# Three elementwise operations moved from GpSimd to VectorE in a two-layer trunk with three attention branches

## Chip, cores and metric

The kernel runs on one core of a Trainium2 chip. The metric is device time in microseconds of one execution; the median of the runs is what counts. Engines are called as the profile calls them: PE is TensorE, DVE is VectorE, ACT is ScalarE, POOL is GpSimd and SP is SyncE, which here only issues DMAs.

## The reference, cut to what matters

Two layers (DEPTH 2) work on x of 1 x 256 x 1024 in float32. Each takes h = RMSNorm(x) and projects it at once to all that the three attention branches need; MoBA has 6 heads, NSA 4, FoX 6, all of 64 columns.

```python
def hybrid_layer(x, ...):
    h = rms_norm(x, norm_g)
    proj = h @ w_in
    ...
    # NSA: per head, three gated outputs are summed (compressed, selected, window)
    return gc[..., 0:1] * o_c + gc[..., 1:2] * o_s + gc[..., 2:3] * o_w
    ...
    y_moba = (o_moba * jax.nn.silu(mz)) @ w_up_moba     # silu(z) = z * sigmoid(z)
    y_nsa = (o_nsa * jax.nn.silu(nz)) @ w_up_nsa
    y_fox = (o_fox * jax.nn.silu(fz)) @ w_up_fox
    g = jax.nn.sigmoid(gl + b_gate).reshape(B, S, N_BRANCH, D_MODEL)
    merged = g[:, :, 0] * y_moba + g[:, :, 1] * y_nsa + g[:, :, 2] * y_fox
    return x + merged @ w_out
```

## The kernel before, in words

The 256 rows are two tiles of 128 partitions (t = 0, 1). Every large product is made in three passes of 32-bit matmuls on split operands: a weight tile `st` comes by DMA on SP's queue, ACT copies it to the high part `wh` (L262), DVE subtracts to get the low part `wl` (L263), and PE runs `wh` with the high activations, `wl` with the high ones, `wh` with the low ones (`mm3`, L287 to L289). Split tiles are prepared four tiles ahead (`prefetch`, `part`).

A layer goes: projections of the branches with their head work; scores, softmax and values of the heads (`attend`) while PE also makes the six gate products (`mm_gl`); then the gate stage (`gate_out`), the lift with the merge (`mm_up`), and the output product (`mm_out`).

The order on PE is written out. Its instructions are emitted by generators on a hand-kept clock (`tick`, `unit`, `finish`, with lags such as LAG_K) and the kernel asks for a manual schedule of PE alone. The instructions of DVE, ACT and POOL are not held to the order in which the code emits them: the framework sorts each of these queues when the program is built, by order of emission among what it takes to be ready. On the chip every queue then runs strictly in that order. The two places where the change and PE meet most closely are a chain and a ring. The chain is in `cmp_heads`: PE transposes the compressed probabilities, DVE copies them to `pc` (L850), PE multiplies them with the values (L857). On DVE's queue the second of two sums on `ck` (L909, which waits for a DMA that goes through DRAM) and a weight split stand ahead of `pc`. The ring is the PSUM pool `pat` of three tiles, all named `at`, which scores (L565, L566), transposes of queries and keys (L473) and transposes of probabilities (L579) use in turn; L494 to L496 read the transposed keys and so free a tile.

Three places work on POOL and are touched. In `gate_out`, for each half c of the 1024 columns and each t, ACT makes the sigmoid of z into a buffer `tmp` (L937), POOL multiplies z by it (L940), DVE multiplies the head outputs `om` by that (L941); PE transposes the products later (`transpose_split`, L336). In `mm_up`, for each half n and branch b, DVE multiplies the accumulator by the gate (L974 for b = 0, L977 for the others) and adds it to `mg` (L978): POOL does so for b = 1, DVE for b = 2. In `gated`, which closes an NSA branch, DVE multiplies the values in the PSUM bank `o` by 1/sum times gate (L666 for the first branch, L670 for the two others), and for these POOL adds the result to `om` (L671). `gated` is called three times in a layer: for the selected branch (first), for the window branch, and in `cmp_heads` for the compressed one. Buffers named `tmp` form a ring of four, which the loads of `b_gate` on SP's queue (L917) use too.

Of the kernel before, what the change touches and what calls it, by code (L numbers as in the profile page):

```python
# [9 lines left out]
F32 = mybir.dt.float32  # L10
F32R = mybir.dt.float32r
AF = mybir.ActivationFunctionType
ALU = mybir.AluOpType
# [3 lines left out]
S, D, L, HD = 256, 1024, 2, 64  # L17
# [5 lines left out]
MH, NH, FH = 6, 4, 6  # L23
# [70 lines left out]
def trunk(ctx, tc, x, w_in, b_gate, cmp_w1, w_up_moba, w_up_nsa, w_up_fox, w_out, gains_d, eye_d, x_t, small_d, row_d, out):  # L94
    nc = tc.nc
    V, A, G, T = nc.vector, nc.scalar, nc.gpsimd, nc.tensor
# [13 lines left out]
    wk = ctx.enter_context(tc.tile_pool(name="wk", bufs=2))  # L110
# [66 lines left out]
    def after(i, others):  # L177

        for o in others:
            tc.add_manual_dep(i.ins, o.ins.name, nosync, reason="one table set after the other")  # L180
# [40 lines left out]
    def finish(*us):  # L221
        while any(u["done"] is None for u in us):
            tick(0.25)
# [67 lines left out]
    def new_acc():  # L291
        return [pacc.tile([128, 512], F32, name="acc") for _ in range(NT)]

    def dense(ps, act, parts, n, half=0, ks=None, order=None, oldest=None):

        whole = ks is not None or len(parts) == KD
        ks = list(ks) if ks is not None else [half * 4 + i for i in range(len(parts))]
        for i, t in order or [(i, t) for i in range(len(parts)) for t in range(NT)]:
            h, lo = part(parts[i], oldest and (oldest if t < NT - 1 else parts[i]))
            k = ks[i]  # L300
            first = i == 0 if whole else k == 0
            last = i == len(parts) - 1 if whole else k == KD - 1
            mm3(ps[t][:, 0:n], block(act, 0, k, t), block(act, 1, k, t), h, lo, first, last)
            tick(3 * n * 0.00042)
# [16 lines left out]
    def new_T():  # L321

        return [(pgs.tile([128, 4, S], F32R, name="hT", tag="page"),
                 pgs.tile([128, 4, S], F32R, name="lT", tag="page")) for _ in range(2)]
# [4 lines left out]
    def transpose_split(dst, t, blocks, gains=None):  # L329

        n = len(blocks)
        h, lo = [d[:, :, t * 128:(t + 1) * 128] for d in dst]
        ps = pat.tile([128, 512], F32, name="at")
        p3 = ps[:, 0:n * 128].rearrange("p (k c) -> p k c", k=n)
        for k in range(n):
            T.transpose(p3[:, k, :], blocks[k], ident)  # L336
        if gains is not None:
            f = wk.tile([128, 4, 128], F32, name="tmp", bufs=4)[:, 0:n]
            V.tensor_tensor(f, p3, gains[:, :, None].to_broadcast([128, n, 128]), op=ALU.mult)
            p3 = f  # L340
        A.activation(h, p3, AF.Copy)
        V.tensor_tensor(lo, p3, h.bitcast(F32), op=ALU.subtract)

    def blocks_of(a, k0, n):
        return [a[:, k * 128:(k + 1) * 128] for k in range(k0, k0 + n)]
# [4 lines left out]
    def layer(l):  # L350
# [307 lines left out]
        def gated(bank, rsum, b, first=False):  # L658

            V.reciprocal(rsum, rsum)  # L660
            V.tensor_tensor(rsum, rsum, sh["ng"].rearrange("p t (h b) -> p t h b", b=3)[:, :, :, b], op=ALU.mult)
            for t in range(NT):
                o = sh["om"][t][:, 384:640].rearrange("p (h d) -> p h d", d=HD)
                g = rsum[:, t, :, None].to_broadcast([128, NH, HD])
                if first:
                    V.tensor_tensor(o, bank[:, t], g, op=ALU.mult)  # L666
                else:
                    tmp = wk.tile([128, 512], F32, name="tmp", bufs=4)
                    o1 = tmp[:, 0:256].rearrange("p (h d) -> p h d", d=HD)
                    V.tensor_tensor(o1, bank[:, t], g, op=ALU.mult)  # L670
                    G.tensor_tensor(o, o, o1, op=ALU.add)  # L671

        def nsa_heads(b, v):
            def head(h, bank, rsum):
                return attend(sh["nqs"][:, h, :], [sh[n][:, b, :] for n in ("kh2", "kl2")], lambda kt: sh[v][:, kt, :],
                              h, bank, h, rsum)
            return group(4, head, lambda bank, rsum: gated(bank, rsum, b + 1, b == 0))
# [146 lines left out]
        def cmp_heads():  # L824
# [31 lines left out]
            for t in range(NT):  # L856
                T.matmul(bank[:, t].rearrange("p h d -> p (h d)"), pcs[t], sh["vcb"].rearrange("p h d -> p (h d)"),  # L857
                         start=True, stop=True)
            gated(bank, wc, 0)
            turn[2] = clock[0] + LAG_B  # L860

# [67 lines left out]
        def gate_out(c):  # L929

            if c == 0:
                sh["oT"] = [tuple(qkp.tile([128, 4, S], F32R, name="qkT") for _ in range(2)) for _ in range(2)]
            for t in range(NT):
                s_ = wk.tile([128, 512], F32, name="tmp", bufs=4)
                zc = sh["z"][t][:, c * 512:(c + 1) * 512]
                oc = sh["om"][t][:, c * 512:(c + 1) * 512]
                i = A.activation(s_, zc, AF.Sigmoid)  # L937
                after(i, exps)
                sigs.append(i)
                G.tensor_tensor(zc, zc, s_, op=ALU.mult)  # L940
                V.tensor_tensor(oc, oc, zc, op=ALU.mult)  # L941
            yield 6.5 + 4.5 * c
            for t in range(NT):
                transpose_split(sh["oT"][c], t, blocks_of(sh["om"][t], c * 4, 4))
                yield 1.0
# [15 lines left out]
        def mm_up(n, parts, before):  # L961

            if n == 0:
                sh["mg"] = [pgs.tile([128, D], F32, name=f"mg{t}", tag="page") for t in range(NT)]
                sh["mT"] = new_T()
            for b, (k0, k1) in enumerate(((0, 3), (3, 5), (5, 8))):
                finish(*before.get(b, ()))
                ps = new_acc()
                dense(ps, sh["oT"], parts[k0:k1], 512, ks=range(k0, k1))
                for t in range(NT):  # L970
                    g = sh["gl"][t][b][:, n * 512:(n + 1) * 512]
                    m = sh["mg"][t][:, n * 512:(n + 1) * 512]
                    if b == 0:
                        V.tensor_tensor(m, ps[t], g, op=ALU.mult)  # L974
                    else:
                        tmp = wk.tile([128, 512], F32, name="tmp", bufs=4)
                        V.tensor_tensor(tmp, ps[t], g, op=ALU.mult)  # L977
                        (G if b == 1 else V).tensor_tensor(m, m, tmp, op=ALU.add)  # L978

        def merged_T(n):  # L980
            yield 3.0
# [90 lines left out]
        def run(starts, following):  # L1072
# [51 lines left out]
            for c in range(5):  # L1124
                mm_gl(c, sh["gls"][c])
            finish(*every)
            g0, g1 = unit(gate_out(0)), unit(gate_out(1))
            unit(gate_sig(0))
            unit(gate_sig(1))
            mm_gl(5, sh["gls"][5])  # L1130
            unit(gate_sig(2))
            mm_up(0, sh["ups"][0], {0: [g0], 1: [g1]})
            m0 = unit(merged_T(0))
            mm_up(1, sh["ups"][1], {})
            m1 = unit(merged_T(1))
            finish(m0)
# [41 lines left out]
```

## Time and profile before

| | |
|---|---|
| median of 3 runs | 518.33 us (518.25 to 518.99) |
| the profiled execution | 517.28 us |
| its span | 515.5 us, 8244 instructions |
| PE busy | 501.9 us, 97% |
| DVE busy | 401.5 us, 78%, 846 instructions |
| ACT busy | 334.6 us, 65% |
| POOL busy | 60.5 us, 12%, 84 instructions |

The profile times single instructions in one execution. The span runs from the first instruction to the last; the execution's own time is 1.8 us longer, and the medians are taken from other executions. An engine's busy time is an average over stages with different limits, so a stage is read from its own stretch. Idle time on an engine is given with what ended it. Consecutive instructions of one kind may stand in one row of the timeline (x2), with the time from the first start to the last end. Durations on an engine can overlap a little: one instruction may start before the one before it is written out.

### The profile page before, as it was taken

The page shows a single profiled execution, that of the slowest core. Times are in us where ns is not written, and L with a number is a line of the kernel's source. Part 1 is how long each engine was busy: PE and PEld are TensorE (multiplying, and loading weights), DVE is VectorE, ACT ScalarE, POOL GpSimd, SP SyncE. Part 2 cuts the span into 40 slices and gives each one's busy share as a digit, 9 for nine tenths or more (in the row PEclk, how much of TensorE's full clock was granted, in tenths as well). Part 3 has the DMA queues.
Part 4 walks back from the last instruction along what each step waited for, and adds up shares of the span by engine and source line. Part 5 has one row for each costly group of instructions (what it writes and reads, how often), then busy time and mean ns, then how long its engine had stood idle before and what let it go on. Part 6 is the DMA issues. An engine that isn't in the chain of part 4 may idle for free.

```text
span 515.5 us, 8244 instructions
## 1 busy us (share of the span) xinstructions
PE 501.9 (97%) x2822; PEld 446.6 (87%) x2822; DVE 401.5 (78%) x846; ACT 334.6 (65%) x645; POOL 60.5 (12%) x84
## 2 busy tenths in 40 slices
PE   8899999999999999999999999999998999999997
PEld 6788999999788888888889989999987888888886
DVE  4799988789876658998497998768997755698953
ACT  4887676976675576654276976678757666655440
POOL 3510211000110005025100000000011000042300
PEclk9999999999999999999999999999999999999999
DMA  8999886555585443756557898647556643537502
GB/s 279 332 243 256 237 246 194 148 166 162 164 257 144 124 129 116 219 163 190 144 145 207 202 244 268 173 127 202 154 182 189 194 130 116 164 117 226 180 9 81
DMA packets 60226, 93.09 MB, mean 181 GB/s; under 512 B 3980, under 2 KB 34840, under 8 KB 60184
## 3 DMA queue, kind: packets, MB, share of 16 engines
q1 hardware_dynamic: 56592, 89.67, 59.7%
q10 hardware_dynamic: 3592, 2.90, 1.7%
q8 instruction: 22, 0.36, 0.3%
q14 instruction: 20, 0.16, 0.1%
HBM read 91.49 MB, written 1.06 MB: 180 GB/s over the span
## 4 chain that ended last, share of the span: by engine, by line
PE 81%; DVE 8%; ACT 5%; DMA 3%; issue 3%; ACTq 0%; DVEq 0%; SPq 0%
PE acc L287 22%; PE acc L289 21%; PE acc L288 21%; DVE wl L263 4%; PE at L579 2%; DMA st<-in_w_in_dram 2%; ACT wh L262 2%; PE at L565 2%; PE at L566 2%; PE at L336 1%; PE o L587 1%; PE o L589 1%; PE o L591 1%; PE at L473 1%; PE o L768 1%
## 5 line engine op out<-in xcount | busy, mean ns | idle before, releaser
L263 DVE TENSOR_TENSOR wl<-st,wh 128x1024 fp32r<-128x1024 f32 (+4 forms) x180 | 200.3, 1120 | 53.7 <-ACT wh L262 52.0
L262 ACT ACTIVATE wh<-st 128x1024 fp32r<-128x1024 f32 (+4 forms) x180 | 170.2, 953 | 86.9 <-PE acc L289 68.0
L287 PE MATMUL acc<-wh,hT 128*128 128x512 f32 (+4 forms) x560 | 216.8, 387 | 1.4 <-ACT wh L262 1.0
L288 PE MATMUL acc<-wl,hT 128*128 128x512 f32 (+4 forms) x560 | 202.6, 362 | 0.9 <-DVE wl L263 0.9
L289 PE MATMUL acc<-wh,lT 128*128 128x512 f32 (+4 forms) x560 | 203.0, 362 | 0.0
L289 PEld LDWEIGHTS acc<-wh,lT 128*128 128x128 f32 x560 | 105.1, 188 | 10.9
L287 PEld LDWEIGHTS acc<-wh,hT 128*128 128x128 f32 x560 | 105.8, 189 | 9.2 <-ACT wh L262 1.4
L288 PEld LDWEIGHTS acc<-wl,hT 128*128 128x128 f32 x560 | 105.9, 189 | 7.8 <-DVE wl L263 1.5
L574 ACT ACTIVATE p<-p,nm 128x128 f32<-128x128 f32 x80 | 35.6, 446 | 24.4 <-DVE nm L572 24.3
L940 POOL TENSOR_TENSOR z<-z,tmp 128x512 f32<-128x512 f32 x8 | 12.9, 1645 | 109.0 <-ACT tmp L937 109.0
L287 PE MATMUL acc<-wh,qkT 128*128 128x512 f32 x64 | 25.6, 400 | 0.0
L289 PE MATMUL acc<-wh,qkT 128*128 128x512 f32 x64 | 25.0, 391 | 0.0
L288 PE MATMUL acc<-wl,qkT 128*128 128x512 f32 x64 | 25.0, 390 | 0.0
L978 POOL TENSOR_TENSOR mg<-mg,tmp 128x512 f32<-128x512 f32 x8 | 15.8, 1997 | 51.5 <-DVE tmp L977 51.5
L579 PE MATMUL at<-ident,p 128*128 128x128 f32 x120 | 19.8, 274 | 0.3
L926 DVE SCALAR_TENSOR_TENSOR gl<-acc,rt,tmp 128x512 f32<-128x512 f32 x24 | 17.3, 745 | 1.8 <-PE o L591 1.1
L579 PEld LDWEIGHTS at<-ident,p 128*128 128x128 f32 x120 | 15.0, 146 | 2.5 <-ACT qkT L496 0.6
L572 DVE CUSTOM_DVE_ANT_0 p<-at,tabs 128x128 f32<-128x128 f32 (+1 forms) x56 | 17.0, 354 | 0.1
L583 DVE COPY pt<-at 128x384 f32<-128x384 f32 x20 | 11.1, 555 | 7.2 <-PE at L579 7.0
L768 PE MATMUL o<-wh,Z 128*63 128x256 f32 x64 | 15.6, 282 | 0.4 <-DVE Z L744 0.3
L581 ACT ACTIVATE pt<-at 128x384 f32<-128x384 f32 x20 | 9.7, 483 | 9.5 <-PE at L579 9.4
L769 PE MATMUL o<-wl,Z 128*63 128x256 f32 x64 | 15.4, 280 | 0.2 <-DVE wl L263 0.2
(238 smaller groups left out, 690.9 us busy)
## 6 DMA issues: line engine op xcount, KB each, us to landing
st<-in_w_in_dram SPq DMA_DIRECT2D x52, 512.0 KB, 3.6
st<-in_w_in_dram SPq DMA_DIRECT2D x56, 384.0 KB, 4.1
st<-in_cmp_w_dram SPq DMA_DIRECT2D x32, 256.0 KB, 4.7
st<-in_w_out_dram SPq DMA_DIRECT2D x16, 512.0 KB, 3.8
st<-in_w_in_dram SPq DMA_DIRECT2D x8, 396.0 KB, 6.9
st<-in_w_in_dram SPq DMA_DIRECT2D x8, 390.0 KB, 3.2
tmp<-in_b_gate_dram SPq DMA_DIRECT2D x12, 256.0 KB, 4.4
st<-in_w_up_moba_dram SPq DMA_DIRECT2D x4, 512.0 KB, 3.6
```

What stands on the lines that cost most here:

```text
L262: return (lambda: A.activation(h, s_, AF.Copy), lambda: V.tensor_tensor(lo, s_, h.bitcast(F32), op=ALU.subtract))
L263: lambda: V.tensor_tensor(lo, s_, h.bitcast(F32), op=ALU.subtract))
L287: T.matmul(ps, sh, wh, start=first, stop=False)
L288: T.matmul(ps, sh, wl, start=False, stop=False)
L289: T.matmul(ps, sl, wh, start=False, stop=last)
L572: V.tensor_tensor_reduce(out=u, in0=sp, in1=add[t], scale=-SCALE, scalar=BIG, op0=ALU.add, op1=ALU.min, accum_out=nm)
L574: exps.append(A.activation(u, u, AF.Exp, bias=nm, scale=-1.0, accum_out=rsum[:, t, hb:hb + 1]))
L579: T.transpose(pts[:, s * 128:(s + 1) * 128], p[:, s * 128:(s + 1) * 128], ident)
L768: T.matmul(U, st, h, start=i == 0, stop=False)
L769: T.matmul(U, st, lo, start=False, stop=i == CL - 1)
L926: V.scalar_tensor_tensor(sh["gl"][t][b][:, n * 512:(n + 1) * 512], ps[t], sh["r"][:, t:t + 1], bg, op0=ALU.mult, op1=ALU.add)
L978: (G if b == 1 else V).tensor_tensor(m, m, tmp, op=ALU.add)
```

## The change

The product of z and its sigmoid, and the sum of the second branch, are given to DVE. The NSA sum becomes one DVE operation per head, which multiplies by the head's factor and adds to `om`; a group of two products on 128x256 and two sums becomes eight operations on 128x64, and its two `tmp` buffers are no longer taken.

```diff
@@ gated
             for t in range(NT):
                 o = sh["om"][t][:, 384:640].rearrange("p (h d) -> p h d", d=HD)
-                g = rsum[:, t, :, None].to_broadcast([128, NH, HD])
                 if first:
-                    V.tensor_tensor(o, bank[:, t], g, op=ALU.mult)
-                else:
-                    tmp = wk.tile([128, 512], F32, name="tmp", bufs=4)
-                    o1 = tmp[:, 0:256].rearrange("p (h d) -> p h d", d=HD)
-                    V.tensor_tensor(o1, bank[:, t], g, op=ALU.mult)
-                    G.tensor_tensor(o, o, o1, op=ALU.add)
+                    V.tensor_tensor(o, bank[:, t], rsum[:, t, :, None].to_broadcast([128, NH, HD]), op=ALU.mult)
+                    continue
+                for h in range(NH):
+                    V.scalar_tensor_tensor(o[:, h], bank[:, t, h], rsum[:, t, h:h + 1], o[:, h], op0=ALU.mult, op1=ALU.add)
@@ gate_out
-                G.tensor_tensor(zc, zc, s_, op=ALU.mult)
+                V.tensor_tensor(zc, zc, s_, op=ALU.mult)
                 V.tensor_tensor(oc, oc, zc, op=ALU.mult)
@@ mm_up
-                        (G if b == 1 else V).tensor_tensor(m, m, tmp, op=ALU.add)
+                        V.tensor_tensor(m, m, tmp, op=ALU.add)
```

## Rows read from the trace of the kernel before

**Rows 1.** The page, busy us (share of the span) and instructions:

```profile
PE 501.9 (97%) x2822; PEld 446.6 (87%) x2822; DVE 401.5 (78%) x846; ACT 334.6 (65%) x645; POOL 60.5 (12%) x84
```

**Rows 2.** PE's waits: who for whom, us in total, times, longest:

```profile
PE o L857 <- DVE pc L850: 2.6, 2, 1.5
```

**Rows 3.** Stretches: length, busy us (instructions) of PE, PEld, DVE, ACT, POOL, clock, DMA:

```profile
126.00:146.00 20.00, 18.81 (x103) 15.38 (x102) 17.41 (x52) 12.54 (x35) 3.19 (x5) 1.00 0.61 192
146.00:196.00 50.00, 50.00 (x289) 43.20 (x289) 30.39 (x68) 32.96 (x67) 0.00 (x0) 1.00 0.52 153
196.00:232.00 36.00, 36.00 (x172) 29.73 (x171) 33.19 (x38) 22.23 (x26) 9.93 (x6) 1.00 0.57 166
232.00:256.00 24.00, 24.00 (x112) 19.88 (x111) 15.91 (x20) 8.52 (x9) 8.95 (x6) 1.00 0.61 179
...
448.00:484.00 36.00, 36.00 (x172) 29.84 (x171) 33.24 (x39) 20.99 (x26) 9.92 (x6) 1.00 0.54 169
```

**Rows 4.** Groups of POOL: busy us, mean ns of one, idle before them:

```profile
L978 POOL TENSOR_TENSOR mg<-mg,tmp 128x512 f32<-128x512 f32 x8 | 15.8, 1997 | 51.5 <-DVE tmp L977 51.5
L940 POOL TENSOR_TENSOR z<-z,tmp 128x512 f32<-128x512 f32 x8 | 12.9, 1645 | 109.0 <-ACT tmp L937 109.0
...
L671 POOL TENSOR_TENSOR om<-om,tmp 128x256 f32<-128x256 f32 x8 | 5.7, 739 | 66.7 <-DVE rs_a L318 54.9 <-DVE tmp L670 11.8
```

**Rows 5.** Timeline, gate stage of the first layer, DVE, then PE (start, us):

```profile
200.13 3.48 DVE L941 TENSOR_TENSOR om<-om,z 128x512 f32<-128x512 f32 x2 [1.19 <-POOL z L940]
...
205.76 1.28 DVE L941 TENSOR_TENSOR om<-om,z 128x512 f32<-128x512 f32 x2
...
210.01 0.60 PE L336 MATMUL at<-ident,om 128*128 128x128 f32 x4
```

**Rows 6.** Timeline, merge of the first layer's first half, DVE, then PE:

```profile
227.36 1.28 DVE L978 TENSOR_TENSOR mg<-mg,tmp 128x512 f32<-128x512 f32 x2
...
229.63 0.60 PE L336 MATMUL at<-ident,mg 128*128 128x128 f32 x4
```

**Rows 7.** DVE's scalar_tensor_tensor from PSUM: two groups, and a timeline row:

```profile
L503 DVE SCALAR_TENSOR_TENSOR kl<-at,tabs,kh 128x128 fp32r<-128x128 f32 x8 | 2.6, 347 | 0.1
...
L871 DVE SCALAR_TENSOR_TENSOR xf<-acc,rt,row 128x6 f32<-128x6 f32 x4 | 0.9, 224 | 1.1 <-PE acc L289 1.1
...
44.27 0.61 DVE L503 SCALAR_TENSOR_TENSOR kl<-at,tabs,kh 128x128 fp32r<-128x128 f32 x2
```

**Rows 8.** Timeline, DVE, second NSA group of the first layer:

```profile
141.75 0.75 DVE L670 TENSOR_TENSOR tmp<-o,wc 128x256 f32<-128x256 f32 x2
```

**Rows 9.** Timeline, first layer: the PSUM ring behind that group:

```profile
140.63 0.55 DVE L583 COPY pt<-at 128x384 f32<-128x384 f32 x1
...
141.23 0.33 PE L565 MATMUL at<-qkT 128*128 128x128 f32 x1 [0.17 <-DVE pt L583]
...
143.40 0.40 ACT L574 ACTIVATE p<-p,nm 128x128 f32<-128x128 f32 x1 [1.98 <-DVE nm L572]
...
152.25 0.58 ACT L496 ACTIVATE qkT<-at,tabs 64x384 fp32r<-64x384 f32 x1 [0.24 <-DVE klT_fk L495]
...
153.79 0.30 PE L565 MATMUL at<-qkT 128*128 128x128 f32 x1
```

**Rows 10.** Timeline, first layer: DVE ahead of `pc`, and PE's wait for it:

```profile
137.09 0.96 DVE L909 TENSOR_TENSOR ck<-ck,tabs 128x768 f32<-128x768 f32 x1 [1.72 <-DMA ck<-csd]
137.96 1.22 DVE L263 TENSOR_TENSOR wl<-st,wh 128x1024 fp32r<-128x1024 f32 x1
139.10 0.48 DVE L850 COPY pc<-at 128x128 f32<-128x128 f32 x2
...
139.44 1.13 PE L857 MATMUL o<-vcb,pc 128*128 128x256 f32 x4 [1.03 <-DVE pc L850]
```

## The prediction

> **What bounds the kernel now.** I read the busy times first. PE is busy 501.9 of 515.5 us, 97%, while POOL, from which the change takes work, is busy 12% [rows 1]. So the end is set by PE's fixed order, and the change can move the time only by opening or closing a gap on PE. The view of PE's own waits comes second: what the reader is to see there is how short it is. Past the start of each layer one entry is left, two waits of PE for `pc` on DVE, 2.6 us in all, the longer 1.5 [rows 2], the shorter 1.03 [rows 10]. Third, the stretches that hold the three edited places. From 146 to 256 us PE is busy all the time, and in the second layer's gate stage again [rows 3]: nothing that DVE or POOL does there ends a wait of PE. Only the stretch from 126 to 146 us, where the NSA sums run, has PE below its whole length, 18.81 of 20.00, with DVE busy 17.41. The NSA sums are therefore the part that can show; the other two sit under a full PE.
>
> **The gate products (eight, L940).** Removed: eight POOL instructions of 1645 ns, 12.9 us of POOL [rows 4], and DVE's 1.19 us of waiting for the first of them in each layer [rows 5]. Added: eight DVE instructions on 128x512 with all operands in SBUF. The nearest row is the same shape and kind at L978, two in 1.28 us [rows 6], 0.68 for one and 0.60 from one start to the next. Per layer that adds 4 x 0.60 = 2.4 us to DVE. Given back: the two L941 that run beside POOL take 3.48 us where the two after it take 1.28 [rows 5], so 2.2 us, and the wait of 1.19. DVE comes through about 1.0 us earlier (1.19 + 2.2 - 2.4). Could it be a loss? The second half's products end at 205.76 + 1.28 = 207.04, and PE does not begin the transposes even of the first half before 210.01 [rows 5]. So 2.97 us of cover stand behind a change of about -1.0, and a gain has no reader, since PE reaches these transposes in its own order with no gap. Term: 0, from above and below. Without that cover a late product would cost PE its whole lateness.
>
> **The sums of the merged branches (eight of sixteen at L978).** Removed: eight POOL instructions of 1997 ns, 15.8 us [rows 4]. Added: 2 x 0.60 = 1.2 us of DVE for each half of the columns. The second branch is added ahead of the third, so the worst is that all 1.2 us come through to the third branch's sums. The first of those ends at 227.36 + 0.68 = 228.04, PE's transposes of `mg` start at 229.63 [rows 6]: 1.59 us of cover. Term: 0. A gain again finds PE full [rows 3]. The hidden side effect, less waiting of weight loads on SP's queue for buffers, shortens nothing that PE waits for. No DMA is added or moved, and POOL, left with its zero fills and rotary tables, gets to them no later.
>
> **The NSA sums (L670, L671).** There are four such groups, two in each layer. Removed per group: two DVE products from PSUM, 0.75 us for two [rows 8], and two POOL sums of 739 ns [rows 4]. Added: eight DVE instructions, each 128x64, one input in PSUM, one in SBUF, a scalar per partition. The trace has this operation at 6 columns (224 ns) and at 128 columns (347 ns) [rows 7]. Between them 64 columns cost 224 + 58 x (347 - 224)/122 = 282 ns. From start to start it is less: two L503 take 0.61 us together [rows 7], 0.08 less than twice 347 ns, so DVE starts the next one 0.08 us before the last ends. I take 0.20 us from one to the next, 1.60 for eight. The two products that go away hold DVE 0.75 - 0.08 = 0.67. **Each group lengthens DVE's queue by 0.93 us.** The bounds: 0.14 us each (224 less 0.08), so 1.15 for eight, +0.5; and 0.282 each with no overlap, 2.26, +1.6. What is queued behind?
>
> The first group of a layer has scores and a weight split behind it, and then `ck` (L909), before which DVE stands idle for 1.72 us, waiting for a DMA, until 137.09 [rows 10]. 0.93, and even 1.6, ends in that idle time, and `wl` and `pc` behind it start when they do now. PE's wait for `pc` stays. Term: 0.
>
> The second group, at 141.75, is behind `pc` and ahead of the scores of two MoBA heads. ACT waits for those (1.98 us before 143.40) and then works its queue off, up to L496 at 152.25, which frees a PSUM tile of the `at` ring at 152.25 + 0.58 = 152.83. PE asks for that tile at 153.79 [rows 9]: 0.96 us later. The hand-over itself takes 0.05: `pt` ends at 140.63 + 0.55 = 141.18 and PE starts at 141.23 [rows 9]. So 0.91 us is free, 0.93 is added: 0.02 us of new wait, 0.04 for the two layers. This is the tightest cover in the change.
>
> [...]
>
> **The sum.** 0 + 0 + 0 + 0.04 = 0.04 us on the profiled execution, 517.28 us (515.5 of span and 1.8 around it), so 517.32. That execution lies 1.05 below the median of the three runs, 518.33. Moved to the median: 518.4 us, no change that shows. About 0.2%, 1.0 us, is what a measurement of this kernel can tell from none.
>
> **Rivals.** First, **slower through the PSUM ring**. If the eight small instructions do not overlap (each waiting for the one before, since all write parts of one `om` tile), a group adds 2.26 - 0.67 = 1.59 us, 0.68 more than the 0.91 free, in both layers: 1.4 us, 519.7. It decides once one instruction takes more than (0.67 + 0.91)/8 = 0.20 us from start to start. Against it: successive instructions overlap in the row at hand [rows 7]. For it: the margin is almost exactly used up. Chance 0.14. [...]
>
> Second, **faster through `pc`**. Only PE's order is written out; DVE's queue is put in order anew when the program is built, from what is then thought ready. In the present order `pc` stands behind `ck`, late by its DMA, and a split `wl` whose place costs 139.10 - 137.96 = 1.14 us [rows 10]. Eight instructions for two can tip that order. If `pc` comes ahead of `wl` in both layers, 1.03 goes whole and at least 1.14 of the 1.5; if ahead of `ck` too, both go: 2.6 us, 515.8. Chance 0.18: the wait is there, but nothing in the edit aims at it.
>
> Third, **slower through `pc`**: the same re-ordering puts one more split, or the second pair of scores, between `ck` and `pc`. Priced at one split, 1.14 in each layer, 2.3 us: 520.7. Chance 0.12.
>
> That the products leave POOL is written in the edit and can't fail to happen. That POOL's share hid something of use, so that the whole 34 us of it came off the span, is ruled out by the full PE [rows 3].
>
> **How the numbers follow.** No change has 0.56, and its own range is 517.9 to 518.9: the lower bound of the small instruction gives 0, the rest is the spread of the runs. Faster has 0.18, slower 0.14 + 0.12 = 0.26. For 8 in 10 the range goes from the faster rival's 515.8 to just past the third rival's 520.7, so 521.0; beyond it lie re-orderings that set several instructions in front of `pc`.
>
> **What would show it.** POOL falls by 12.9 + 15.8 + 5.7 = 34 us to about 26. DVE's L941 are all 0.68 us. The small instructions read about 0.28 us, eight of them 1.7 us from the first start to the last end. PE's waits still list `pc` with about 2.6 us, and L565 after each second group starts without a new wait. In the gate stage PE is busy all the time, with the transposes at the same distance. A time off by over 1 us means that `pc`'s entry has changed, or that a wait for a PSUM tile of the `at` ring has come up near 154 us and at its counterpart in the second layer; a new gap under the gates or the sums would prove the cover there misread.

## The result: 1.0% slower, and the profile after

The changed kernel takes 523.74 us, the median of 4 runs (522.43 to 524.82), against 518.34: a ratio of 1.010, 95% interval 1.0073 to 1.0128. The forecast was 518.4, no change, with 515.8 to 521.0 as its range; the result lies outside. The profiled execution took 522.43 us with a span of 520.6, so 5.15 us more than the one of before.

The page's busy times, to be held against [rows 1]:

```profile
PE 505.0 (97%) x2822; PEld 450.0 (86%) x2822; DVE 404.8 (78%) x886; ACT 334.6 (64%) x645; POOL 26.3 (5%) x60
```

POOL has lost its 34 us and stands at the 26 forecast. DVE has gained only 3.3 us. Neither tells why PE is later. PE's own waits do (us in total, times, longest):

```profile
PE at L579 <- DVE nm L572: 6.1, 2, 3.4
```

The two waits for `pc` of [rows 2] are gone from the list. In their place PE waits twice for `nm` at L579, the transposes of probabilities: 6.1 us where it was 2.6. The stretches of [rows 3], with the same columns, and the second layer's counterpart of the first one as the fifth row:

```profile
126.00:146.00 20.00, 17.30 (x88) 14.09 (x88) 15.75 (x53) 9.93 (x25) 0.31 (x1) 0.91 0.54 165
146.00:196.00 50.00, 50.00 (x286) 43.04 (x286) 32.19 (x78) 34.53 (x75) 0.00 (x0) 1.00 0.47 134
196.00:232.00 36.00, 36.00 (x171) 29.85 (x170) 31.01 (x42) 20.89 (x24) 0.00 (x0) 1.00 0.57 181
232.00:256.00 24.00, 24.00 (x115) 19.91 (x115) 19.35 (x24) 10.78 (x12) 4.50 (x4) 1.00 0.57 164
378.00:398.00 20.00, 16.63 (x96) 13.61 (x94) 16.29 (x51) 11.14 (x27) 0.00 (x0) 1.00 0.52 158
448.00:484.00 36.00, 36.00 (x173) 29.96 (x173) 29.92 (x40) 19.85 (x24) 0.00 (x0) 1.00 0.54 177
```

The gate stages and the merge (146 to 256, 448 to 484) still have PE busy from end to end. Only the stretches around the NSA sums got worse: PE is busy for 17.30 of 20.00 us where it was 18.81, and in the second layer for 16.63 where the kernel before had 18.31:

```profile
378.00:398.00 20.00, 18.31 (x98) 15.02 (x96) 16.92 (x49) 12.60 (x35) 2.87 (x4) 1.00 0.62 193
```

Of the six stretches of the kernel after, the first alone has a granted clock (the last column but two) below 1.00, at 0.91.

What DVE does in that stretch, from its timeline (start, us; lines in the changed part stand three lower than in the kernel before, so `ck` is L906, `pc` L847, the product with it L854):

```profile
133.23 0.85 DVE L668 SCALAR_TENSOR_TENSOR om<-o,rsum,om 128x64 f32<-128x64 f32 x4
134.15 0.96 DVE L906 TENSOR_TENSOR ck<-ck,tabs 128x768 f32<-128x768 f32 x1
135.03 0.28 DVE L572 CUSTOM_DVE_ANT_0 p<-at,tabs 128x128 f32<-128x128 f32 x1
...
135.24 0.42 DVE L572 CUSTOM_DVE_ANT_0 p<-at,tabs 128x256 f32<-128x256 f32 x1
...
137.79 0.96 DVE L906 TENSOR_TENSOR ck<-ck,tabs 128x768 f32<-128x768 f32 x1 [2.13 <-DMA ck<-csd]
138.67 0.28 DVE L572 CUSTOM_DVE_ANT_0 p<-at,tabs 128x128 f32<-128x128 f32 x1
...
138.88 0.42 DVE L572 CUSTOM_DVE_ANT_0 p<-at,tabs 128x256 f32<-128x256 f32 x1
139.22 0.08 DVE L572 DVE_READ_ACCUMULATOR2_ANT nm<- 128x1 f32 x1
```

And PE in the same stretch:

```profile
139.45 0.52 PE L579 MATMUL at<-ident,p 128*128 128x128 f32 x3 [2.70 <-DVE nm L572]
...
144.57 0.31 PE L565 MATMUL at<-qkT 128*128 128x128 f32 x1
```

In the kernel before, DVE's timeline reads:

```profile
131.82 0.28 DVE L572 CUSTOM_DVE_ANT_0 p<-at,tabs 128x128 f32<-128x128 f32 x1
...
132.52 0.41 DVE L572 CUSTOM_DVE_ANT_0 p<-at,tabs 128x256 f32<-128x256 f32 x1
...
133.85 0.96 DVE L909 TENSOR_TENSOR ck<-ck,tabs 128x768 f32<-128x768 f32 x1
134.73 0.28 DVE L572 CUSTOM_DVE_ANT_0 p<-at,tabs 128x128 f32<-128x128 f32 x1
...
134.94 0.42 DVE L572 CUSTOM_DVE_ANT_0 p<-at,tabs 128x256 f32<-128x256 f32 x1
```

There the scores of a first head (A, two instructions of L572, at 131.82 and 132.52) ran ahead of the first sum on `ck`, and those of a second head (B, at 134.73 and 134.94) ahead of the second sum, which waits for its DMA [rows 10]. Now the eight small instructions fill the place where A's stood, A's scores have slipped behind the first sum, and B's behind the second: B's two start only at 138.67 and 138.88. PE had made all four scores by 131.69, yet DVE stood idle for 2.13 us ahead of the second sum and took up B's only behind it, in the order of its queue. PE transposes A's probabilities at L579 into a tile of the three-tile `at` ring, and B's scores hold a tile of that ring until DVE has read them. The last read of B releases PE at 139.45. A's own probabilities can't be what is late: its scores were through on DVE at 135.66 and its exponentials on ACT at 136.48, three microseconds earlier. That B's tile is the one waited for is read from the releaser, the tile's name and the order in which the ring is taken; a ring of four was not tried, but the last experiment, in which A's scores are all early and only one of B's is late, bears it out.

Where the 5.1 us of the span come up, by the start of PE's L565 (the first of a pair of heads' scores) at four places; the last column is the changed kernel with its `ck` sums behind `pc`, an experiment below:

| PE reaches | before | after | later by | late `ck` sums |
|---|---|---|---|---|
| layer 1, the scores ahead of the stretch | 129.80 | 130.53 | 0.73 | 129.51 |
| layer 1, the scores behind `pc` | 140.65 | 144.57 | 3.92 | 139.07 |
| layer 2, ahead | 381.13 | 384.69 | 3.56 | 379.10 |
| layer 2, behind | 392.48 | 397.98 | 5.50 | 388.66 |
| end of the span | 515.5 | 520.6 | 5.1 | 511.3 |

The first 0.73 arises before any changed line; up to there DVE, ACT and POOL have their instructions in the same order in both kernels. In layer 1 the stretch gives 3.19: the wait is 2.70 where it was 1.03, and the clock did the rest (last section). In layer 2 it gives 1.94: 3.37 where it was 1.52, at a granted clock of 1.00. About 0.35 comes back behind each stretch, where the wait for `pt` at L565 [rows 9] is gone.

### The profile page after: what moved, and what is told of

Read it like the earlier page. It is cut to its first block, busy times and chain, and to the rows that moved or that the text cites. A ratio compares the mean times of both kernels' runs of the same rounds, so it can differ in the third digit from the quotient of the medians.

```text
span 520.6 us, 8219 instructions
## 1 busy us (share of the span) xinstructions
PE 505.0 (97%) x2822; PEld 450.0 (86%) x2822; DVE 404.8 (78%) x886; ACT 334.6 (64%) x645; POOL 26.3 (5%) x60
## 4 chain that ended last, share of the span: by engine, by line
PE 80%; DMA 7%; DVE 5%; ACT 5%; issue 2%; ACTq 0%; DVEq 0%; SPq 0%
PE acc L287 22%; PE acc L289 21%; PE acc L288 21%; DMA st<-in_w_in_dram 3%; DMA ck<-csd 3%; DVE wl L263 2%; PE at L579 2%; ACT wh L262 2%; PE at L565 2%; PE at L336 1%; PE at L566 1%; PE o L587 1%; PE at L473 1%; PE o L591 1%; PE o L589 1%
## 5 line engine op out<-in xcount | busy, mean ns | idle before, releaser
L263 DVE TENSOR_TENSOR wl<-st,wh 128x1024 fp32r<-128x1024 f32 (+4 forms) x180 | 196.0, 1093 | 55.7 <-ACT wh L262 53.9
L287 PE MATMUL acc<-wh,hT 128*128 128x512 f32 (+4 forms) x560 | 217.8, 389 | 1.3 <-ACT wh L262 1.2
L289 PE MATMUL acc<-wh,lT 128*128 128x512 f32 (+4 forms) x560 | 204.3, 365 | 0.0
L289 PEld LDWEIGHTS acc<-wh,lT 128*128 128x128 f32 x560 | 106.0, 189 | 11.1
L287 PEld LDWEIGHTS acc<-wh,hT 128*128 128x128 f32 x560 | 106.6, 190 | 9.3 <-ACT wh L262 1.6
L579 PE MATMUL at<-ident,p 128*128 128x128 f32 x120 | 19.9, 274 | 6.4 <-DVE nm L572 6.1
L287 PE MATMUL acc<-wh,qkT 128*128 128x512 f32 x64 | 25.6, 400 | 0.0
L289 PE MATMUL acc<-wh,qkT 128*128 128x512 f32 x64 | 25.0, 391 | 0.0
L579 PEld LDWEIGHTS at<-ident,p 128*128 128x128 f32 x120 | 14.9, 146 | 9.1 <-issue 6.9
L572 DVE CUSTOM_DVE_ANT_0 p<-at,tabs 128x128 f32<-128x128 f32 (+1 forms) x56 | 16.9, 352 | 0.1
L444 ACT ACTIVATE sq<-acc,rt 128x384 f32<-128x384 f32 (+2 forms) x28 | 13.6, 487 | 2.3 <-DVE ss L445 1.7
L574 ACT ACTIVATION_READ_ACCUMULATOR p<-p,nm 128x1 f32 x80 | 14.9, 187 | 0.0
```

Source lines behind the costliest of these rows:

```text
L263: lambda: V.tensor_tensor(lo, s_, h.bitcast(F32), op=ALU.subtract))
L287: T.matmul(ps, sh, wh, start=first, stop=False)
L289: T.matmul(ps, sl, wh, start=False, stop=last)
L444: A.activation(sq, ps[t][:, col:col + nh * HD], AF.Square, scale=sh["r"][:, t:t + 1])
L572: V.tensor_tensor_reduce(out=u, in0=sp, in1=add[t], scale=-SCALE, scalar=BIG, op0=ALU.add, op1=ALU.min, accum_out=nm)
L574: exps.append(A.activation(u, u, AF.Exp, bias=nm, scale=-1.0, accum_out=rsum[:, t, hb:hb + 1]))
```

## Experiments

In the expectations, ORDER is the theory just told, that DVE's queue was sorted anew and head B's scores fell behind a sum that waits for a DMA; GATES puts the loss on DVE's added work in the gate stage and the merge.

**The NSA sums alone.** The kernel before with only the first hunk of the change, everything else left on POOL.

```diff
+                for h in range(NH):
+                    V.scalar_tensor_tensor(o[:, h], bank[:, t, h], rsum[:, t, h:h + 1], o[:, h], op0=ALU.mult, op1=ALU.add)
```

> Kernel before with the NSA edit alone; gate products and merge sums stay on POOL. Theory ORDER (the eight operations push the scores of two MoBA head pairs behind the two sums on ck in DVE's queue, and ck waits for a DMA): PE's wait for the scores (L579 on nm) is 2.5 to 3.5 us in each layer, the time 522 to 524.5 us, like the changed kernel. Theory GATES (the 2.4 and 1.2 us of DVE work added per stage of gates and merge delay PE): 518 to 519 us, no such wait. Theory LENGTH (the NSA operations cost their own 0.9 us of DVE per group, wherever they stand): at most 4 x 0.9 above before, 518.3 to 522, with waits of under 1 us each.

Measured: 523.97 us (521.04 to 525.70), ratio 1.0102 (1.0056 to 1.0148), so the whole loss. Its DVE timeline, then PE's waits:

```profile
133.94 0.96 DVE L909 TENSOR_TENSOR ck<-ck,tabs 128x768 f32<-128x768 f32 x1
134.81 0.28 DVE L572 CUSTOM_DVE_ANT_0 p<-at,tabs 128x128 f32<-128x128 f32 x1
...
137.78 0.96 DVE L909 TENSOR_TENSOR ck<-ck,tabs 128x768 f32<-128x768 f32 x1 [2.33 <-DMA ck<-csd]
138.65 0.28 DVE L572 CUSTOM_DVE_ANT_0 p<-at,tabs 128x128 f32<-128x128 f32 x1
```

```profile
PE at L579 <- DVE nm L572: 5.8, 2, 2.9
```

The same order and the same wait as in the full change.

**The gate products and the merge sums alone.** The other two hunks.

```diff
-                G.tensor_tensor(zc, zc, s_, op=ALU.mult)
+                V.tensor_tensor(zc, zc, s_, op=ALU.mult)
...
-                        (G if b == 1 else V).tensor_tensor(m, m, tmp, op=ALU.add)
+                        V.tensor_tensor(m, m, tmp, op=ALU.add)
```

> Kernel before with the gate products and the merge sums on DVE; the NSA sums stay as before. ORDER: 517.5 to 519 us, PE's wait for pc stays at about 2.6 us, PE is full in the gate stages. GATES: 522 to 524.5 us with waits of PE between 196 and 256 us. LENGTH of NSA: 517.5 to 519 too, so this run tells GATES from the two others.

Measured: 518.54 us over 10 runs, ratio 1.0001 (0.9985 to 1.0017). PE's waits list `pc` as before, and the gate stage and the merge are full (PE 36.00 of 36.00 and 24.00 of 24.00):

```profile
PE o L857 <- DVE pc L850: 2.9, 2, 1.7
```

```profile
196.00:232.00 36.00, 36.00 (x173) 29.83 (x173) 32.97 (x44) 21.76 (x26) 0.00 (x0) 1.00 0.53 166
232.00:256.00 24.00, 24.00 (x111) 19.91 (x110) 17.20 (x22) 8.85 (x10) 4.50 (x4) 1.00 0.61 180
```

GATES is out, and the two covers of the prediction hold: DVE's last gate product ends 3.19 us ahead of PE's first transposes of `om` (2.97 in the kernel before), and the third branch's first sum 1.84 us ahead of those of `mg` (1.59).

**The order alone, without the change.** The kernel before, all work on POOL as it was; the scores of heads A and B are told to stand behind the first and second sum on `ck` (`after` sets an order in the queue and adds no wait on a result).

```diff
+            behind = sh["behind"].pop(0) if sh.get("behind") and not bias else None
...
-                V.tensor_tensor_reduce(out=u, in0=sp, in1=add[t],
+                i = V.tensor_tensor_reduce(out=u, in0=sp, in1=add[t],
                                        scale=-SCALE, scalar=BIG, op0=ALU.add, op1=ALU.min, accum_out=nm)
+                if behind:
+                    after(i, [behind])
...
-                V.tensor_tensor(sh["ck"][:, :, i:i + 128], sh["ck"][:, :, i:i + 128], mask, op=ALU.add)
+                sh.setdefault("behind", []).append(V.tensor_tensor(sh["ck"][:, :, i:i + 128], sh["ck"][:, :, i:i + 128], mask, op=ALU.add))
```

> Kernel before with one thing added: the scores of the two MoBA heads are made to stand behind the first and the second sum on ck in DVE's queue, an order without a wait of its own. Nothing of the change is in it. ORDER: 521 to 524.5 us, PE waits at L579 for the scores by 1.5 to 3.5 us in each layer. LENGTH and GATES: 518 to 519 us.

Measured: 524.52 us (521.30 to 526.32), ratio 1.0109 (1.0071 to 1.0147). PE's waits (L582 and L573 are L579 and L572 here):

```profile
PE at L582 <- DVE nm L573: 5.4, 2, 2.8
```

The order by itself makes the loss, with none of the small instructions in the kernel. (DVE's queue is not that of the changed kernel in every place: a weight split stands ahead of the second sum here, behind B's scores there.) So the order is enough; that nothing of the loss stays without it is shown two runs further down. The profiled span is 8.0 us longer than before; 3.28 of it come up in the first stretch and 4.46 in the second, more than the added waiting, since the granted clock fell behind both gaps, to 0.91 and 0.88 on the mean of the two stretches (last section).

**The `ck` sums on POOL.** The changed kernel, with the two sums taken out of DVE's queue.

```diff
-                V.tensor_tensor(sh["ck"][:, :, i:i + 128], sh["ck"][:, :, i:i + 128], mask, op=ALU.add)
+                G.tensor_tensor(sh["ck"][:, :, i:i + 128], sh["ck"][:, :, i:i + 128], mask, op=ALU.add)
```

> Changed kernel with the two sums on ck (L909) given to POOL, so that DVE's queue holds nothing that waits for that DMA; the eight NSA operations stay. ORDER: the wait for the scores goes, and pc's wait with it, PE has no wait between 126 and 146 us: 515 to 517.5 us, granted clock 1.0 there. LENGTH: the operations are all still there, so at least 521 us. A cost of the small operations themselves would leave a wait at the scores of over 0.5 us.

Measured: 520.22 us over 10 runs (517.10 to 522.36), ratio 1.0036 (1.0011 to 1.0061): better than the change, but 2.7 us above the upper end of what was expected. PE's waits, then ACT's and PE's timeline:

```profile
PE at L473 <- ACT pt L581: 5.1, 2, 2.6
```

```profile
140.97 1.49 ACT L562 ACTIVATE bias<-ck,cq 128x256 f32<-128x256 f32 x4 [3.77 <-POOL ck L909]
...
143.71 0.47 ACT L581 ACTIVATE pt<-at 128x384 f32<-128x384 f32 x1
```

```profile
144.23 0.55 PE L473 MATMUL at<-ident,qn 128*128 128x128 f32 x3 [2.52 <-ACT pt L581]
```

The scores' wait is gone, and the same late DMA has stopped another queue: ACT's bias instructions need `ck`, stand ahead of `pt` in ACT's order, and `pt` frees the ring's tile. On POOL the second sum itself took 2.92 us, and ended later for it. The granted clock, expected at 1.0, was 0.98 in the stretch. The expectation had followed the DMA on DVE only.

**The `ck` sums emitted later.** The changed kernel; the generator yields once more before the sums, so that the sort finds the scores first.

```diff
+            yield 1.5
             mask = tabs[:, K_MASK + 128:K_MASK + 256][:, None, :].to_broadcast([128, FH, 128])
```

> Changed kernel; the two sums on ck are emitted 1.5 us of the hand-kept clock later, so that all four scores of the MoBA heads stand ahead of both sums in DVE's queue again; pc stays behind them, as in the kernel before. ORDER: PE's wait for the scores (L579 on nm) is gone, a wait for pc of 2.5 to 5 us in all comes back, the time is that of the kernel before or little above it, 517.5 to 520.5 us. LENGTH (the eight small operations cost by themselves): 522 us or more, whatever stands ahead of what.

Measured: 515.58 us (514.29 to 515.61), ratio 0.9939 (0.9921 to 0.9958), lower than the 517.5 to 520.5 expected. DVE's timeline:

```profile
134.24 0.28 DVE L572 CUSTOM_DVE_ANT_0 p<-at,tabs 128x128 f32<-128x128 f32 x1
...
134.79 1.22 DVE L263 TENSOR_TENSOR wl<-st,wh 128x1024 fp32r<-128x1024 f32 x1
135.93 0.95 DVE L910 TENSOR_TENSOR ck<-ck,tabs 128x768 f32<-128x768 f32 x1
137.68 0.96 DVE L910 TENSOR_TENSOR ck<-ck,tabs 128x768 f32<-128x768 f32 x1 [0.81 <-DMA ck<-csd]
138.56 0.48 DVE L850 COPY pc<-at 128x128 f32<-128x128 f32 x2
```

All scores are through before the first sum, as expected. What the expectation left out: the split `wl` has moved ahead too and is done while the DMA is on its way, so `pc` follows the second sum directly, at 138.56 where it was 139.10, and of PE's waits for `pc` 0.4 us is left.

**The `ck` sums behind `pc`, in both kernels.** The same two edits on the kernel after and on the kernel before.

```diff
-                V.tensor_copy(pc, pt[:, 0:128])
+                sh.setdefault("pc", []).append(V.tensor_copy(pc, pt[:, 0:128]))
...
+            yield 9.0
...
-                V.tensor_tensor(sh["ck"][:, :, i:i + 128], sh["ck"][:, :, i:i + 128], mask, op=ALU.add)
+                after(V.tensor_tensor(sh["ck"][:, :, i:i + 128], sh["ck"][:, :, i:i + 128], mask, op=ALU.add), sh["pc"])
```

On the kernel after (e6):

> Changed kernel; the sums on ck are emitted 9 us of the hand-kept clock later and kept behind the copies to pc, so that neither DVE nor ACT has a reader of that DMA ahead of work that PE needs soon. ORDER: no wait of PE for scores, pc or pt between 126 and 146 us and in its counterpart: 515.4 us (518.0 less the 2.6 of pc), between 514.5 and 516.5, granted clock 1.0 in that stretch. LENGTH: at least 521 us. If a small wait stays it is for a PSUM tile of the ring, under 0.7 us per layer.

On the kernel before:

> Kernel before with the same two lines as e6: sums on ck late and behind pc; nothing of the change. ORDER: also 515.4 us, between 514.5 and 516.5, within 0.3% of e6, so that the change itself is worth nothing either way once the DMA is out of the way. If the change is worth something by itself, e6 and b6 differ by more than 0.3%.

Measured: 514.16 us (513.07 to 515.57), ratio 0.9921 (0.9906 to 0.9937), with the change, and 513.97 us (512.80 to 516.28), ratio 0.9919 (0.9899 to 0.9939), without it. Both beat both kernels. The stretches with the change:

```profile
126.00:146.00 20.00, 20.00 (x113) 16.84 (x112) 18.35 (x63) 12.40 (x32) 0.31 (x1) 1.00 0.66 203
...
378.00:398.00 20.00, 20.00 (x111) 17.00 (x110) 18.51 (x56) 12.96 (x33) 0.00 (x0) 1.00 0.59 183
```

and DVE's timeline, where the two sums run late and wait for nothing:

```profile
143.34 1.81 DVE L910 TENSOR_TENSOR ck<-ck,tabs 128x768 f32<-128x768 f32 x2
```

PE has no gap left in either stretch. With the order held, no difference that the change makes shows: the intervals cover each other. The table's last column accounts for the 4.2 us of span against the kernel before: 0.29 ahead of the stretches, 1.29 and 1.79 in them, 0.45 and 0.38 behind them. Inside the stretches it is the waits for `pc`, 1.03 and 1.52, with some 0.27 each around them (the product behind the wait took 1.13 where it takes 1.02 here); behind them most of it is the wait for `pt`, which had put off an L565 by 0.33 in each layer.

**The sums on DVE in the wide form.** The kernel before, with all three kinds of work on DVE but the NSA sums as two instructions of 256 columns for each tile, the product as it was and an addition. The other two places are edited as in the change.

```diff
-                    G.tensor_tensor(o, o, o1, op=ALU.add)
+                    V.tensor_tensor(o, o, o1, op=ALU.add)
```

> Kernel before with all three parts on DVE, but the NSA sum as two wide operations per group and tile pair (product and sum over 256 columns), not one per head. In its DVE queue the first sum on ck stands ahead of all scores of the two heads, the second ahead of the very last score alone. ORDER: the first transposes (L579) need only scores that stand ahead of the second sum and wait by under 1 us; pc is behind one more score than before: waits of 2.5 to 4.5 us in all, 518 to 520.5 us. A cost of the small form itself (eight against four operations): 518 us or less, with pc's wait unchanged at 2.6.

Measured: 522.95 us (520.06 to 524.04), ratio 1.0081 (1.0055 to 1.0107), above the 518 to 520.5 expected. DVE's timeline, then PE's:

```profile
135.10 0.42 DVE L572 CUSTOM_DVE_ANT_0 p<-at,tabs 128x256 f32<-128x256 f32 x1
...
135.45 0.28 DVE L572 CUSTOM_DVE_ANT_0 p<-at,tabs 128x128 f32<-128x128 f32 x1
...
137.14 0.96 DVE L909 TENSOR_TENSOR ck<-ck,tabs 128x768 f32<-128x768 f32 x1 [1.40 <-DMA ck<-csd]
138.01 0.42 DVE L572 CUSTOM_DVE_ANT_0 p<-at,tabs 128x256 f32<-128x256 f32 x1
```

```profile
138.58 0.52 PE L579 MATMUL at<-ident,p 128*128 128x128 f32 x3 [1.96 <-DVE nm L572]
...
142.12 0.30 PE L565 MATMUL at<-qkT 128*128 128x128 f32 x1
```

In this layer only the larger half of head B's scores has slipped behind the second sum, and that is enough: PE's transposes start when the last reader of B's tile is done. In the second layer the first load of `ck` is late too, and DVE stands idle for 3.08 us ahead of its sum. DVE's timeline, then PE's:

```profile
388.33 0.96 DVE L909 TENSOR_TENSOR ck<-ck,tabs 128x768 f32<-128x768 f32 x1 [3.08 <-DMA ck<-csd]
```

```profile
389.90 0.33 PE L848 MATMUL at<-ident,uc 128*128 128x128 f32 x1 [2.35 <-DVE nm L572]
```

There A's scores, behind the first sum, come late as well, and PE waits for A's tile already at L848, the transposes that `pc` copies, and 0.89 more at L579. The expectation had asked of the second sum alone how late it is. All this fits the reading of the ring, and shows that the loss does not need the small form of the operation.

## Why the prediction was wrong

**The step that failed** is the one on the first NSA group: "0.93, and even 1.6, ends in that idle time, and `wl` and `pc` behind it start when they do now. PE's wait for `pc` stays. Term: 0." It added durations to a queue whose order it took as fixed. The durations did fit: the last small instruction of the group ends at 134.08, and DVE still stands idle for 2.13 us ahead of the second sum on `ck`. But B's scores, which had run ahead of that idle time, now stand behind it. The term was not 0 but, with what the clock added, 3.2 us in the first layer and 1.9 in the second, less 0.35 that came back behind each. That the order is enough for this is shown by the run that forces it on the kernel before, and that the added work costs nothing without it by the runs with the `ck` sums moved back in DVE's queue.

Two readings of that step were off as well. Between the group and the second sum there is no weight split on DVE; there is the first sum on `ck`, which needs a DMA too. And the step asked only for `pc`. B's scores ended at 134.94 + 0.42 = 135.36, and PE took up their tile, for L579, at 135.85: 0.49 us of cover on the ring, about half of the 0.93 added. No run shows what that cover would have cost with the order kept as it was.

**The rival that came nearest** is the third, slower through a re-ordering that puts "one more split, or the second pair of scores, between `ck` and `pc`". The second pair of scores did go there. But the wait was sought at `pc`, and PE meets the scores earlier, at L579 through the ring; and the price, 1.14 a layer for one split, was that of an instruction, where the late DMA sets it: 1.67 and 1.85 us more of waiting, and the clock. The prediction had said that DVE's queue is sorted anew when the program is built and still gave a fixed order 0.56.

**What held.** The gate products and the merge sums cost nothing, as the run with them alone shows. A size was off without effect: the gate products were to come through about 1.0 us earlier, and came 0.2 earlier against PE (3.19 us of cover for 2.97). In the changed kernel the rows by form (busy us, mean ns) are:

```profile
L938 DVE TENSOR_TENSOR om<-om,z 128x512 f32<-128x512 f32 x8 | 5.5, 684 | 0.0
L937 DVE TENSOR_TENSOR z<-z,tmp 128x512 f32<-128x512 f32 x8 | 5.3, 685 | 0.0
L668 DVE SCALAR_TENSOR_TENSOR om<-o,rsum,om 128x64 f32<-128x64 f32 x16 | 3.9, 278 | 0.0
```

The gate products (L937) and those of `om` (L938) are at 0.68, and the small instruction at 0.278 against the 0.282 worked out. Eight of them in a row, behind the second group's product in DVE's timeline:

```profile
144.53 1.63 DVE L668 SCALAR_TENSOR_TENSOR om<-o,wc,om 128x64 f32<-128x64 f32 x8 [1.43 <-PE o L854]
```

1.63 us from the first start to the last end is (1.63 - 0.28)/7 = 0.193 from one start to the next, where eight durations of 0.278 would make 2.2 us; 0.20 was taken. So the instructions overlap though four at a time write one tile, and the first rival falls: no new wait for the ring comes up at L565, and PE is busy all of 146 to 196, here and in the run with the `ck` sums emitted later, which gets there without the late scores.

**The prediction's own sign for being wrong** was the right place to look: `pc`'s entry has changed. It has gone, which taken alone would have read as the second rival, faster. The other sign, a ring wait near 154 us, named the right ring and the wrong place on it.

## What to carry to other kernels

Where only one engine's order is written out, adding instructions to another's queue can re-sort it, so ask first which instruction of that queue waits for a DMA, who could slip behind it, and what buffers those hold; price that by how late the DMA is, not by the added busy time. An instruction whose input comes late and whose result nobody needs yet belongs late in its queue: two small edits that did this here were worth 0.8%, with the change or without it. Moving the late instruction to another engine helps only in part (520.22 us, still above the kernel before) if that engine's followers stand in front of something PE needs.

## What the runs showed of the hardware

**The clock after a gap.** Two stretches of the kernel after, layer 1, in the columns of the stretches above:

```profile
138.00:142.00 4.00, 2.55 (x9) 2.09 (x10) 4.00 (x10) 2.77 (x9) 0.00 (x0) 0.78 0.13 15
142.00:146.00 4.00, 4.00 (x21) 3.48 (x20) 2.57 (x10) 1.55 (x2) 0.31 (x1) 0.80 0.76 245
```

Behind PE's gap of 2.70 us the granted clock is 0.78 and 0.80 on the mean of each stretch: it stands at 1.00 up to 140.2, at 0.50 from 140.4 to 143.6 and at 1.00 again from 143.8. A product of 128x512 (L287 to L289) takes 0.63 us there and 0.39 at 1.00. From L579 to L565 PE took 139.45 to 144.57, 5.12 us; the wide form did the same instructions at a granted clock of 1.00 in 142.12 - 138.58 = 3.54. The lower clock behind the gap cost 1.58 us, about as much as the added wait itself, 1.67. Not every gap had one behind it: behind the longer gap of layer 2, 3.37 us, the granted clock stayed at 1.00 in the same execution, and with the order forced it fell behind gaps of 2.66 and 2.75 us, to 0.91 and 0.88 on the mean of 126 to 146 and 378 to 398 us, where the same instructions took 5.12 and 5.92. What decides it was not tried.

**The start of the program.** The 0.73 us before the stretches is not put down to the change: the granted clock was 0.80 from 16 to 24 us in that execution and 1.00 in the one of before, but it was 0.82 there in the run that only forces the order, and 1.00 in the run with the NSA sums alone.

**A DMA through DRAM.** In the kernel after, the second of the two loads of `ck` from `csd` (768 KB) is issued at 130.79, takes 7.0 us from issue to landing, and its sum starts at 137.79; the first (384 KB) takes 3.8 us, and 3.9 in the second layer. There no landing of the second load is recorded; its sum starts 7.9 us after the issue. Every wait for scores, `pc` or `pt` told of here hangs on one of these loads. On POOL the second sum took 2.92 us in the first layer, against 0.96 on DVE; both sums together took 4.76 there and 4.58 in the second.
